# Rotary embedding on one core: ScalarE's copies and casts go to VectorE, GpSimd and the DMA queue

## The chip, the core and the metric

The kernel runs on one core of a Trainium2 chip. The metric is the device time of one execution in microseconds (us); the time of a kernel is the median of its runs. Three runs of the kernel before gave 316.24, 316.26 and 316.33 us.

## The reference

The input x has the shape 8 x 2048 x 16 x 64 (batch, position, head, element) in fp32. In each head the 64 elements are 32 pairs; pair i at position s is rotated by the table entries cos[s, i] and sin[s, i]:

```python
x1 = x_pairs[..., 0]
x2 = x_pairs[..., 1]
out1 = x1 * cos - x2 * sin
out2 = x1 * sin + x2 * cos
out = np.stack([out1, out2], axis=-1).reshape(batch, seq_len, num_heads, head_dim)
```

One of the 8 batches is 2048 x 1024 fp32 values, 8.39 MB. All of x is read once (67.1 MB) and an output of the same size is written once; the two tables are 0.26 MB each.

## The kernel before, in words

Position s = 16 p + k lies in partition p, row k of 16, so a batch is 128 partitions x 16 rows x 1024 elements, and each partition's 64 KB of a batch lie in one piece in DRAM. The data is held in SBUF as bf16. The tile `xt` has five homes of one batch each (32 KB a partition); batches 0 to 4 take homes 0 to 4, batches 5, 6 and 7 take homes 0, 1 and 2 again, once batches 0, 1 and 2 are stored.

All large transfers are issued by GpSimd (POOL in the profile) on one queue, and the DMA engines convert between fp32 in DRAM and bf16 in SBUF on the way: `load(b, n)` (line 63) brings in n batches, `store(b, n)` (line 67) takes n batches out. SyncE (SP) issues two transfers on its own queue, which does not convert: the head, the first 4 rows of batch 0 (line 92), and the tail, the last 4 rows of batch 7 (line 133). Both pass as fp32 through a staging tile `st`, and ScalarE (ACT) casts them (lines 101 and 132).

`rotate(b, k0, k1)` is three VectorE (DVE) instructions: qt = x times the sine table (line 82), x = x times the cosine table, in place (line 83), and x plus the pair-swapped qt, in place (line 88). Batch 0 is rotated in two parts (4 rows and 12 rows), every other batch in one. There is one work buffer, which `head`, `qt` and `tail` share in turn.

The order of the work is written out by hand; each engine follows the program's order, and a waiting instruction holds up everything behind it on its engine. What GpSimd does, in this order:

1. The loads of batch 0 (12 rows, line 93), cos and sin (lines 94, 95), batches 1 and 2 in one, batch 3 (both line 63), 14 rows of batch 4 (line 98) and its last 2 rows (line 99).
2. The store of batch 0 (line 67). Two ScalarE copies of one element hold it: line 111 reads an element of the 14 rows of batch 4, so it waits until these have landed, and line 112 rewrites the first element of batch 0 in place, so that the store has to wait for it.
3. `mark` (line 116), a GpSimd copy of the last element of batch 4, which waits for that load. It stands ahead of the store of batches 1 and 2.
4. The store of batches 1 and 2, the load of batch 5 (into home 0, so it waits until batch 0 is stored), the load of batches 6 and 7 (homes 1 and 2, so it waits for the store of batches 1 and 2).
5. The store of batches 3 and 4, the store of batches 5 and 6, and the first 12 rows of batch 7 (line 127).

At the end ScalarE's line 131 writes one element of batch 6's home, so that it waits until the store of batches 5 and 6 is done; then line 132 casts the tail, and SyncE stores it (line 133).

Of the kernel before, what the change touches and what calls it, by code (L numbers as in the profile page):

```python
# [2 lines left out]

# [4 lines left out]


@with_exitstack  # L10
def kernel(
    ctx: ExitStack,
    tc: tile.TileContext,
    x: bass.AP,
    cos: bass.AP,
    sin: bass.AP,
    out: bass.AP,
):
    nc = tc.nc
    fp32 = mybir.dt.float32  # L20
    bf16 = mybir.dt.bfloat16
    mult = mybir.AluOpType.mult
    add = mybir.AluOpType.add

    B, S, H, D = x.shape
    P = 128
    K = S // P
    KP = 16
    D2 = D // 2
    HD = H * D  # L30
    NX = 5
    HEAD = 4
    TAIL = 4
    LAST = 2


    HOME = [0, 1, 2, 3, 4, 0, 1, 2]

    x_t = x.rearrange("b (p k) h d -> b p k (h d)", p=P, k=K)
    out_t = out.rearrange("b (p k) h d -> b p k (h d)", p=P, k=K)  # L40
    x_r = x.rearrange("b (p k) h d -> p b (k h d)", p=P, k=K)
    out_r = out.rearrange("b (p k) h d -> p b (k h d)", p=P, k=K)
    cos_t = cos.rearrange("(p k) c -> p (k c)", p=P, k=K)
    sin_t = sin.rearrange("(p k) c -> p (k c)", p=P, k=K)

    consts = ctx.enter_context(tc.tile_pool(name="consts", bufs=1))
    stage = ctx.enter_context(tc.tile_pool(name="stage", bufs=1))

    xt = consts.tile([P, NX, K * HD], bf16)
    cos_sb = consts.tile([P, K * D2], fp32)  # L50
    sin_sb = consts.tile([P, K * D2], fp32)
    c_tab = consts.tile([P, K, D], bf16)
    s_tab = consts.tile([P, K, D], bf16)

    gate = consts.tile([1, 1], bf16)
    mark = consts.tile([1, 1], bf16)

    def home(b, k0=0, k1=K):
        return xt[:, HOME[b], k0 * HD : k1 * HD].rearrange("p (k c) -> p k c", c=HD)

    def load(b, n):
        h = HOME[b]
        nc.gpsimd.dma_start(out=xt[:, h : h + n], in_=x_r[:, b : b + n])  # L63

    def store(b, n):
        h = HOME[b]
        nc.gpsimd.dma_start(out=out_r[:, b : b + n], in_=xt[:, h : h + n])  # L67

    def rotate(b, k0=0, k1=K):
        nk = k1 - k0  # L70
        xp = home(b, k0, k1)
        qt = stage.tile([P, KP, HD], bf16, name="qt", tag="work")

        def rows(a):
            return a.rearrange("p k (h e) -> p k h e", h=H, e=D)

        def tab(a):
            return dataclasses.replace(
                a, offset=a.offset + k0 * D, ap=[a.ap[0], [D, nk], [0, H], [1, D]]
            )  # L80

        nc.vector.tensor_tensor(out=rows(qt[:, :nk]), in0=rows(xp), in1=tab(s_tab), op=mult)  # L82
        nc.vector.tensor_tensor(out=rows(xp), in0=rows(xp), in1=tab(c_tab), op=mult)  # L83
        q_swap = dataclasses.replace(
            qt, offset=qt.offset + 1, ap=[qt.ap[0], [2, nk * HD // 2], [-1, 2]]
        )
        x3 = xp.rearrange("p k (a j) -> p (k a) j", j=2)
        nc.vector.tensor_tensor(out=x3, in0=x3, in1=q_swap, op=add)  # L88

    with tc.manual_schedule():  # L90
        head = stage.tile([P, TAIL, HD], fp32, name="st", tag="work")
        nc.sync.dma_start(out=head[:, :HEAD], in_=x_t[0, :, :HEAD])
        nc.gpsimd.dma_start(out=home(0, HEAD), in_=x_t[0, :, HEAD:])  # L93
        nc.gpsimd.dma_start(out=cos_sb, in_=cos_t)  # L94
        nc.gpsimd.dma_start(out=sin_sb, in_=sin_t)  # L95
        load(1, 2)
        load(3, 1)
        nc.gpsimd.dma_start(out=home(4, 0, K - LAST), in_=x_t[4, :, : K - LAST])  # L98
        nc.gpsimd.dma_start(out=home(4, K - LAST), in_=x_t[4, :, K - LAST :])  # L99

        nc.scalar.copy(out=home(0, 0, HEAD), in_=head[:, :HEAD])  # L101
        s2 = s_tab.rearrange("p k (i j) -> p (k i) j", j=2)
        nc.vector.tensor_copy(out=s2[:, :, 0], in_=sin_sb)  # L103
        nc.vector.tensor_scalar_mul(s2[:, :, 1], sin_sb, -1.0)  # L104
        nc.vector.tensor_copy(  # L105
            out=c_tab.rearrange("p k (i j) -> p (k i) j", j=2),
            in_=cos_sb.to_broadcast([P, K * D2, 2]),
        )
        rotate(0, 0, HEAD)
        rotate(0, HEAD, K)  # L110
        nc.scalar.copy(out=gate, in_=home(4, K - LAST - 1, K - LAST)[:1, 0, :1])  # L111
        nc.scalar.copy(out=xt[:1, HOME[0], :1], in_=xt[:1, HOME[0], :1])  # L112
        store(0, 1)
        rotate(1)
        rotate(2)
        nc.gpsimd.tensor_copy(out=mark, in_=xt[:1, 4, K * HD - 1 :])  # L116
        store(1, 2)
        load(5, 1)
        load(6, 2)
        rotate(3)  # L120
        rotate(4)
        store(3, 2)
        for b in range(5, B):
            rotate(b)
            if b == 6:
                store(5, 2)
        nc.gpsimd.dma_start(out=out_t[B - 1, :, : K - TAIL], in_=home(B - 1, 0, K - TAIL))  # L127

        tail = stage.tile([P, TAIL, HD], fp32, name="st", tag="work")
        last = home(B - 1, K - TAIL, K)  # L130
        nc.scalar.copy(out=xt[:1, HOME[B - 2], :1], in_=xt[:1, HOME[B - 1], K * HD - 1 :])  # L131
        nc.scalar.copy(out=tail, in_=last)  # L132
        nc.sync.dma_start(out=out_t[B - 1, :, K - TAIL :], in_=tail)


# [1 line left out]
_INS = ['x', 'cos', 'sin']  # L137
_OUTS = [((8, 2048, 16, 64), 'float32')]


# [23 lines left out]
```

## Time and profile before

The profile is of one execution. Times in it are us from its first instruction.

| What | Value |
|---|---|
| median of the three runs | 316.26 us |
| span of the profiled execution, first to last instruction | 314.4 us |
| what lies around the span (median less span) | 1.8 us |
| DVE busy | 210.4 us, 30 instructions |
| ACT busy | 8.9 us, 6 instructions |
| POOL busy | 13.9 us, 19 instructions |
| DMA packets, bytes counted in the profile | 2816, 102.24 MB |
| share of the 16 DMA engines' span: GpSimd's queue, SyncE's queue | 96.8%, 3.3% |
| one rotation of a full batch (lines 82, 83, 88) | 3 x 8.69 us |
| ScalarE cast of the head, of the tail | 3.60 us each |
| GpSimd copy `mark` | 5.01 us |
| issue of one GpSimd transfer | 0.54 to 0.74 us |

How to read it: a DMA appears in three places. Its issue is a short instruction on the queue's engine (POOL, or SPq for SyncE); the page's last part gives the time from issue to landing; and the rows "GB/s" and "DMA" tell what the 16 DMA engines did meanwhile. Bytes are counted on the bf16 side for a converting load and on the fp32 side for a store, so that about 215 GB/s while loading and 430 GB/s while storing are the same pace in fp32 bytes. A window of the trace counts a DMA packet wholly where it starts.

### The profile page before, as it was taken

What the parts mean: (1) busy time and instruction counts of PE and PEld (TensorE: products, weight loads), DVE (VectorE), ACT (ScalarE), POOL (GpSimd) and SP (SyncE); (2) the same over time, 40 slices, a digit from 0 to 9 for tenths busy, and PEclk for the clock granted to TensorE, in tenths of its full rate; (3) what the DMA queues carried; (4) which work ended last, traced back from release to release, by engine and by line L of the source; (5) the groups of instructions that cost most, each with busy time, mean ns of one, the idle gap of its engine ahead of it and who ended that gap; (6) DMA issues with size and microseconds to landing.
All of it is one profiled execution on the core that took longest, in us unless ns stands there. A gap on an engine that the chain in (4) does not pass through costs nothing.

```text
span 314.4 us, 116 instructions
## 1 busy us (share of the span) xinstructions
DVE 210.4 (67%) x30; ACT 8.9 (3%) x6; POOL 13.9 (4%) x19
## 2 busy tenths in 40 slices
DVE  0009995099999999999992399903999999200000
ACT  1040000000000000000000000000000000000400
POOL 5000000000002400000000000000000000000000
DMA  7999999999999999999999999999999999999997
GB/s 254 263 283 200 200 200 267 200 200 213 229 233 258 425 509 400 400 459 475 400 200 246 221 200 200 254 213 333 400 525 409 400 400 525 409 400 400 434 434 333
DMA packets 2816, 102.24 MB, mean 325 GB/s; under 512 B 256, under 2 KB 256, under 8 KB 512
## 3 DMA queue, kind: packets, MB, share of 16 engines
q0 software_dynamic: 2528, 98.04, 96.8%
q1 hardware_dynamic: 288, 4.19, 3.3%
HBM read 67.63 MB, written 67.11 MB: 429 GB/s over the span
## 4 chain that ended last, share of the span: by engine, by line
another core or an unknown queue 87%; DMA 5%; ACT 1%; ACTq 1%; issue 0%
DMA st<-in_x_dram 5%; ACT xt L101 1%; ACTq L159 1%; ACT xt L131 0%; ACT xt L112 0%; ACTq L131 0%; ACT gate L111 0%
## 5 line engine op out<-in xcount | busy, mean ns | idle before, releaser
L82 DVE TENSOR_TENSOR qt<-xt,s_tab 128x16384 bf16<-128x16384 bf16 (+2 forms) x9 | 69.7, 7743 | 34.4 <-DMA xt<-in_x_dram 34.3
L83 DVE TENSOR_TENSOR xt<-xt,c_tab 128x16384 bf16<-128x16384 bf16 (+2 forms) x9 | 69.7, 7744 | 0.4
L88 DVE TENSOR_TENSOR xt<-xt,qt 128x16384 bf16<-128x16384 bf16 (+2 forms) x9 | 69.7, 7744 | 0.3
L103 DVE CAST s_tab<-sin_sb 128x512 bf16<-128x512 f32 x1 | 0.5, 458 | 23.8 <-DMA sin_sb<-in_sin_dram 23.8
L67 POOL DMA_DIRECT2D out_dram<-xt x4 | 2.7, 671 | 185.5 <-ACT xt L112 93.8
L131 ACT COPY xt<-xt 1x1 bf16<-1x1 bf16 x1 | 0.2, 193 | 195.4 <-DMA out_dram<-xt 195.4
L116 POOL COPY mark<-xt 1x1 bf16<-1x1 bf16 x1 | 5.0, 5014 | 1.4 <-DMA xt<-in_x_dram 1.4
L63 POOL DMA_DIRECT2D xt<-in_x_dram x4 | 2.6, 656 | 43.0 <-DMA out_dram<-xt 43.0
L101 ACT CAST xt<-st 128x4096 bf16<-128x4096 f32 x1 | 3.6, 3604 | 13.3 <-DMA st<-in_x_dram 13.3
L132 ACT CAST st<-xt 128x4096 f32<-128x4096 bf16 x1 | 3.6, 3598 | 0.0
L111 ACT COPY gate<-xt 1x1 bf16<-1x1 bf16 x1 | 0.2, 193 | 79.7 <-DMA xt<-in_x_dram 79.7
L127 POOL DMA_DIRECT2D out_dram<-xt x1 | 0.6, 572 | 25.5 <-DVE xt L88 25.5
L101 ACT ACT_TABLE_LOAD x1 | 1.3, 1283 | 0.7 <-PEq L148 0.7
L93 POOL DMA_DIRECT2D xt<-in_x_dram x1 | 0.7, 680 | 0.8 <-PEq L159 0.8
L105 DVE CAST c_tab<-cos_sb 128x1024 bf16<-128x1024 f32 x1 | 0.7, 684 | 0.0
L99 POOL DMA_DIRECT2D xt<-in_x_dram x1 | 0.6, 592 | 0.0
L98 POOL DMA_DIRECT2D xt<-in_x_dram x1 | 0.6, 586 | 0.0
L95 POOL DMA_DIRECT2D sin_sb<-in_sin_dram x1 | 0.6, 562 | 0.0
L94 POOL DMA_DIRECT2D cos_sb<-in_cos_dram x1 | 0.6, 554 | 0.0
L104 DVE TENSOR_SCALAR s_tab<-sin_sb 128x512 bf16<-128x512 f32 x1 | 0.4, 445 | 0.0
L112 ACT COPY xt<-xt 1x1 bf16<-1x1 bf16 x1 | 0.2, 189 | 0.0
L148 POOL MEMSET const-float32-0.0<- 128x1 f32 x1 | 0.1, 93 | 0.2 <-issue 0.2
(3 smaller groups left out, 0.3 us busy)
## 6 DMA issues: line engine op xcount, KB each, us to landing
xt<-in_x_dram POOLq DMA_DIRECT2D x2, 8192.0 KB, 58.5
xt<-in_x_dram POOLq DMA_DIRECT2D x2, 4096.0 KB, 67.6
out_dram<-xt POOLq DMA_DIRECT2D x1, 6144.0 KB, 40.9
xt<-in_x_dram POOLq DMA_DIRECT2D x1, 3584.0 KB, 94.3
xt<-in_x_dram POOLq DMA_DIRECT2D x1, 3072.0 KB, 21.2
st<-in_x_dram SPq DMA_DIRECT2D x1, 2048.0 KB, 14.5
out_dram<-st SPq DMA_DIRECT2D x1, 2048.0 KB, 15.5
xt<-in_x_dram POOLq DMA_DIRECT2D x1, 512.0 KB, 96.3
```

The source lines that it names most:

```text
L63: nc.gpsimd.dma_start(out=xt[:, h : h + n], in_=x_r[:, b : b + n])
L67: nc.gpsimd.dma_start(out=out_r[:, b : b + n], in_=xt[:, h : h + n])
L82: nc.vector.tensor_tensor(out=rows(qt[:, :nk]), in0=rows(xp), in1=tab(s_tab), op=mult)
L83: nc.vector.tensor_tensor(out=rows(xp), in0=rows(xp), in1=tab(c_tab), op=mult)
L88: nc.vector.tensor_tensor(out=x3, in0=x3, in1=q_swap, op=add)
L93: nc.gpsimd.dma_start(out=home(0, HEAD), in_=x_t[0, :, HEAD:])
L94: nc.gpsimd.dma_start(out=cos_sb, in_=cos_t)
L101: nc.scalar.copy(out=home(0, 0, HEAD), in_=head[:, :HEAD])
L105: nc.vector.tensor_copy(out=c_tab.rearrange("p k (i j) -> p (k i) j", j=2), in_=cos_sb.to_broadcast([P, K * D2, 2]),)
L116: nc.gpsimd.tensor_copy(out=mark, in_=xt[:1, 4, K * HD - 1 :])
L132: nc.scalar.copy(out=tail, in_=last)
L159: with _tile.TileContext(nc) as tc:
```

## The change

- The head's cast (line 101) is an instruction of VectorE, at the same place of the program.
- Batch 4 is loaded by one DMA on GpSimd's queue, not by two (14 rows and 2 rows).
- The two ScalarE copies that hold the first store are gone. In their place GpSimd copies the last element of batch 3 (home 3) ahead of the store, so the store waits, behind that copy on its own engine, until the load of batch 3 has landed.
- Batch 7 is stored by one DMA on GpSimd's queue. The tail's two ScalarE instructions, its staging tile and SyncE's transfer are gone; the 12-row store of line 127 becomes one of 16 rows at the same place.
- The loop over the last three batches is written out, in the same order. ScalarE has no instruction left.

```diff
-        head = stage.tile([P, TAIL, HD], fp32, name="st", tag="work")
+        head = stage.tile([P, HEAD, HD], fp32, name="st", tag="work")
...
-        nc.gpsimd.dma_start(out=home(4, 0, K - LAST), in_=x_t[4, :, : K - LAST])
-        nc.gpsimd.dma_start(out=home(4, K - LAST), in_=x_t[4, :, K - LAST :])
+        load(4, 1)
 
-        nc.scalar.copy(out=home(0, 0, HEAD), in_=head[:, :HEAD])
+        nc.vector.tensor_copy(out=home(0, 0, HEAD), in_=head[:, :HEAD])
...
         rotate(0, 0, HEAD)
         rotate(0, HEAD, K)
-        nc.scalar.copy(out=gate, in_=home(4, K - LAST - 1, K - LAST)[:1, 0, :1])
-        nc.scalar.copy(out=xt[:1, HOME[0], :1], in_=xt[:1, HOME[0], :1])
+        nc.gpsimd.tensor_copy(out=gate, in_=xt[:1, 3, K * HD - 1 :])
         store(0, 1)
...
-        for b in range(5, B):
-            rotate(b)
-            if b == 6:
-                store(5, 2)
-        nc.gpsimd.dma_start(out=out_t[B - 1, :, : K - TAIL], in_=home(B - 1, 0, K - TAIL))
-
-        tail = stage.tile([P, TAIL, HD], fp32, name="st", tag="work")
-        last = home(B - 1, K - TAIL, K)
-        nc.scalar.copy(out=xt[:1, HOME[B - 2], :1], in_=xt[:1, HOME[B - 1], K * HD - 1 :])
-        nc.scalar.copy(out=tail, in_=last)
-        nc.sync.dma_start(out=out_t[B - 1, :, K - TAIL :], in_=tail)
+        rotate(5)
+        rotate(6)
+        store(5, 2)
+        rotate(7)
+        store(7, 1)
```

More of the change, by code (lines that the diff above doesn't have):

```diff
@@ L32 @@
     HEAD = 4
-    TAIL = 4
-    LAST = 2
     HOME = [0, 1, 2, 3, 4, 0, 1, 2]
```

## The prediction

> **What bounds the kernel now.** I read the page's head and slices first, then the six DMA issues with their landings, then the busy time by stage, and last the timeline around the first store.
>
> ```profile
> span 314.4 us, 116 instructions
> DVE 210.4 (67%) x30; ACT 8.9 (3%) x6; POOL 13.9 (4%) x19
> ...
> DMA  7999999999999999999999999999999999999997
> ...
> HBM read 67.63 MB, written 67.11 MB: 429 GB/s over the span
> ```
>
> No engine is near its span, but the DMA row is 9 in all slices but the first and last. So the 16 DMA engines set the time: 134.7 MB in 314.4 us. The windows below are cut at landings: batch 3 loaded, batch 4 loaded (two DMAs), batches 1 and 2 stored, 3 and 4 stored, 5 and 6 stored, and batch 7 stored (two DMAs). The columns are window, length, busy time of DVE, ACT, POOL, clock, DMA share, GB/s.
>
> ```profile
> 62.40:81.70 19.30, 19.16 (x3) 0.00 (x0) 0.00 (x0) 1.00 0.99 214
> 81.70:101.10 19.40, 19.33 (x3) 0.29 (x2) 0.55 (x2) 1.00 1.03 247
> 121.00:159.40 38.40, 38.13 (x6) 0.00 (x0) 0.59 (x2) 1.00 1.02 423
> 217.00:255.60 38.60, 38.45 (x5) 0.00 (x0) 0.70 (x1) 1.00 1.02 435
> 255.60:294.20 38.60, 13.70 (x2) 0.00 (x0) 0.57 (x1) 1.00 1.00 428
> 294.20:313.60 19.40, 0.00 (x0) 3.69 (x2) 0.00 (x0) 1.00 0.92 392
> ```
>
> Every batch costs 19.2 to 19.4 us, loaded or stored, whole or in two pieces: 16 of these are 310 us, and the rest is the start and the end. VectorE waits for loads at 62.5, 178.4 and 217.0, and no transfer starts late. The last row's share of 0.92 isn't a hole: a window counts a packet where it starts, and 16 packets of 48 KB, 0.79 MB, had started just before 294.2 (19.4 us x 392 GB/s is 7.6 MB of the 8.39). In the trace's packet records 15 or 16 engines have a packet in flight from 2.3 us to 312.8 us. The queue serves its DMAs in the order of issue: the store of batches 3 and 4 is issued at 167.55, behind a load issued at 159.37, and lands 88.1 us later, at 255.6, 38.6 us after that load's 217.0. So a transfer issued early waits its turn, and all that counts is that each is issued before the queue runs dry. **An edit is worth only what it changes in DMA bytes, in cost per packet, or in a queue run dry.**
>
> **The change part by part.**
>
> *Head's cast on VectorE.* Removed: one ACT cast, 3.60 us (line 101), at 15.29. Added: a 128x4096 fp32 to bf16 cast on VectorE. No row shows that; the nearest are the DVE casts of 512 and 1024 elements, 0.458 and 0.684 us. Their difference gives 0.44 ns an element, so 2.0 us; 4 x 0.684 is 2.7 us; ACT's 3.60 is the upper end. I take 2.7: 15.3 to 18.0. VectorE's next instruction waits for sin until 23.84, and the rotation after it ends at 51.8, 10.7 us before batch 1 lands. Cost 0; even at 3.6 us it would end at 18.9.
>
> *Batch 4 in one DMA.* One issue less on POOL (0.59 us, at 4.78, nothing behind it): 0. In the queue, the packet records give per engine 8 packets every 2.112 us and 8 every 0.305 us, 19.33 us, where batch 3 has 8 every 2.412 us, 19.30 us. With one pair of end marks less this is **-0.05 us**; the rows' landings (19.4 against 19.3) say -0.1. Rotation 4 starts at 141.0, so the landing at about 101 isn't waited for by VectorE.
>
> *The gate.* The two ACT copies at 98.61 and 98.70 go; a GpSimd copy comes ahead of the first store.
>
> ```profile
> 79.93 8.69 DVE L88 TENSOR_TENSOR xt<-xt,qt 128x16384 bf16<-128x16384 bf16 x1
> 88.65 8.69 DVE L82 TENSOR_TENSOR qt<-xt,s_tab 128x16384 bf16<-128x16384 bf16 x1
> 97.38 8.69 DVE L83 TENSOR_TENSOR xt<-xt,c_tab 128x16384 bf16<-128x16384 bf16 x1
> ...
> 99.19 0.54 POOL L67 DMA_DIRECT2D out_dram<-xt  x1 [93.81 <-ACT xt L112]
> 101.10 5.01 POOL L116 COPY mark<-xt 1x1 bf16<-1x1 bf16 x1 [1.37 <-DMA xt<-in_x_dram]
> 106.11 8.69 DVE L88 TENSOR_TENSOR xt<-xt,qt 128x16384 bf16<-128x16384 bf16 x1
> ```
>
> The mark copies one element and takes 5.01 us: it begins within line 83 (97.38 to 106.07) and ends at 106.11, when that instruction has ended. So a GpSimd copy waits for the VectorE instruction in progress. The new gate waits for batch 3, issued at 3.7 and landing 78.0 us later, at 81.7, within line 88 of rotation 1. At best it takes some 0.2 us as on ACT (81.9); as the mark did, it ends at 88.65. I take 88.65, then 0.54 us of issue. Before, the store was issued at 99.19 and its first packets ran on from batch 4's last at 100.4 to 100.8, so the queue did not run dry; now it is queued 10 us earlier behind batch 4. Cost 0, cover 10 us. The Trainium skill (SBUF — State Buffer, Who interferes with whom) says that a VectorE instruction with two SBUF inputs and a GpSimd instruction that reads SBUF exclude each other, and whichever comes second is blocked until the first ends. By this rule the change swaps two ScalarE copies that wait for nobody for a blocked one; the sum stays, since 88.65 is in time.
>
> Behind the gate on POOL: the store's issue, the mark, and all later transfers. The mark still waits for batch 4 (101.0) and gets through at 106.1, the next store still waits for line 88 at 114.80, and its turn in the queue is 120. The load of batch 5 waits for the first store's landing, 121.0, with a turn at 158. All as before. If a copy makes VectorE wait instead, the row above prices it at 0.04 us (106.07 to 106.11), against 5 us of cover.
>
> *Batch 7 in one DMA.* The ACT copy, the 3.60 us cast, the SP issue and SyncE's 2 MB transfer go; the 12-row store, issued at 269.63, becomes 16 rows. Its turn comes at 293.5, so the earlier work is covered by 24 us. In the packet records the latest engine needs 19.39 us for batch 7 in two pieces (48 KB packets every 1.81 us, 16 KB ones every 0.61); eight whole 64 KB packets, one every 2.41 us and the last one's 2.45, make 19.31: **-0.07 us**. The end waits for a landing on GpSimd's queue, not SyncE's. From the last packet's end to the landing SyncE's took 0.3 us (313.23 to 313.55), GpSimd's 12-row store the same (310.19 to 310.53): 0, with bounds of -0.2 and +0.2 from the rounding of these.
>
> **Sum.** -0.05 - 0.07 = -0.12 us on a span of 314.4; the 1.8 us around it contain nothing that changes. On the median: **316.26 - 0.12 = 316.15 us**, no change within what this kernel's measurement can tell (0.2%, 0.63 us).
>
> **The rivals.**
>
> *The gate comes through late (slower).* If the copy doesn't get in between two VectorE instructions at 88.65, it is tried again at 97.35, which is just in time, and at 106.1, which isn't. From 99.5 on the queue runs dry at 100.7: copy to 106.1, issue from 106.4, first packet about 1.2 us after it (99.19 to 100.4, an upper bound), 107.6: +6.9 us, **323.1 us**. For it: VectorE runs without a gap from 62.5 to 167. Against it: the mark got in at the first border. 0.08.
>
> *The early store shares the DMA engines with batch 4 (slower).* If both were served in turn, batch 4 would land near 120 rather than 101, the mark behind it would end with the VectorE instruction in progress at 123.5, and the store of batches 1 and 2 would go out then, its packets from about 124.7 into a queue empty since 120.5: +4.2 us, **320.5 us**. Against it: the store issued at 167.55 took its turn. 0.05.
>
> *Fewer DMAs save more (faster).* If the 0.92 in the last window is waste, 8% of 19.4 us returns, 1.5 us: **314.7 us**. Against it: the packet records have no holes, and batch 4's last 512 KB landed 2.5 us after its first part (4.26 + 94.3, then 4.78 + 96.3), where one eighth of 19.3 us is 2.4. The Trainium skill (DMA: Bandwidth & Descriptors, Anatomy of one DMA — SWDGE) gives a DMA on this path a fixed cost of about 2.0 us besides its bytes; if that held in a full queue, two DMAs less would save 4 us, an estimate of 312.3. The 0.1 us beside it says that the fixed part is latency here, which the queue hides. 0.07.
>
> **How the numbers follow.** The forecast has 0.80, its own range 315.4 to 316.9: the sum's -0.12, the end's 0.2 either way, and some 0.4 for a small shift at one of the three changed places. This is also the range, as the rivals left out hold 0.20. Of the forecast's 0.80 I put 0.03 beyond 0.63 us on the fast side and 0.02 on the slow side: faster 0.10, same 0.75, slower 0.15.
>
> **What would show it.** Right: ACT's row gone; a DVE cast of about 2 to 3 us at 15.3; the gate's copy from 81.7 to 88.65 and the first store's issue by 89.5; the mark at 101 to 106.1 and the issue at 115.1 unchanged; load 5 issued at 121; DMA row all 9s, batch 7 landing 19.3 to 19.4 us after batch 6. Wrong: the gate at 97 or 106, a hole in the DMA row near 101 to 108, batch 4 landing much later than 101, or an end that comes more than 0.5 us after the last packet.

## The result, and the profile after

The changed kernel takes 317.64 us (median of 5 runs, 317.51 to 317.85) against 316.26 us: 1.0042 times the kernel before, 95% interval 1.0031 to 1.0053. It is **1.4 us slower**, where no measurable change was forecast, and outside the range given. The profiled execution has a span of 315.9 us where before had 314.4.

Line numbers of the changed kernel are 2 lower than before's in `rotate`, `load` and `store` (lines 80, 81, 86, 61, 65); the gate is line 108, the mark line 112. The page's head and DMA row look as before:

```profile
span 315.9 us, 106 instructions
...
DVE 212.6 (67%) x31; POOL 19.1 (6%) x19
...
DMA  8999999999999999999999999999999999999996
```

ScalarE is gone, and the DMA row still has 9 everywhere but at the ends. The packet records (the trace's start and length of every DMA packet) show no hole: from 5.5 to 312 us an engine is without a packet for 0.03 us on average, as in the kernel before. The windows cut at landings, as in the prediction (batch 4 loaded, batch 0 stored, batches 1 and 2 stored, 3 and 4 stored, 5 and 6 stored, 7 stored; with no ACT column now):

```profile
81.70:102.10 20.40, 20.33 (x3) 7.41 (x2) 1.00 1.00 231
102.10:121.50 19.40, 19.33 (x3) 4.67 (x2) 1.00 1.01 432
121.50:160.20 38.70, 38.39 (x6) 0.56 (x1) 1.00 1.01 420
218.00:256.70 38.70, 38.51 (x5) 0.71 (x1) 1.00 1.01 434
256.70:295.30 38.60, 13.65 (x2) 0.57 (x1) 1.00 1.02 435
295.30:314.60 19.30, 0.00 (x0) 0.00 (x0) 1.00 0.89 380
```

One stage has grown: batch 4's load takes 20.4 us where it took 19.4. All later stages are what they were, to 0.1 us. To the hundredth, batch 4 lands at 102.09 (before 101.04: +1.05) and the stores of batches 5 and 6 at 295.28 (294.23: +1.05). The last packet ends at 314.21 (313.23: +0.98, so batch 7 in one DMA is 0.07 us cheaper). From the last landing to the end of the span there are 1.30 us (314.57 to 315.88), where there were 0.86 (313.57 to 314.43: +0.44). 0.98 and 0.44 are the whole difference of 1.4 us. There are **two losses**, at different places.

The timeline around the gate is what the prediction expected:

```profile
81.72 6.92 POOL L108 COPY gate<-xt 1x1 bf16<-1x1 bf16 x1 [76.87 <-DMA xt<-in_x_dram]
88.59 0.54 POOL L65 DMA_DIRECT2D out_dram<-xt  x1
...
102.14 3.95 POOL L112 COPY mark<-xt 1x1 bf16<-1x1 bf16 x1 [13.01 <-DMA xt<-in_x_dram]
```

The gate's copy waits for VectorE and ends in the gap at 88.6, and the store is issued 12 us before its turn. What follows isn't. Narrower windows of the changed kernel (the last column, GB/s, and the share before it count packets where they start) show the last packets of batch 4's load:

```profile
95.40:97.80 2.40, 2.37 (x2) 0.00 (x0) 1.00 1.01 218
97.80:98.30 0.50, 0.50 (x1) 0.00 (x0) 1.00 6.84 1049
98.30:101.10 2.80, 2.80 (x1) 0.00 (x0) 1.00 0.00 0
101.10:101.90 0.80, 0.80 (x1) 0.00 (x0) 1.00 3.07 1311
```

All 16 engines start their last packet of the load between 97.8 and 98.3, and the next one, the first of the store, only after 101.1, not 2.4 us later. By the packet records these last packets take 3.09 to 3.61 us where the seven before them take 2.43; the mean excess is 1.0 us. (Excess or stretch, from here on: by how much these last packets are longer than packets of their size elsewhere, on average over the 16 engines.) There is no hole: the engines are "busy" all along, only slower. The next place where a store lies queued behind a load is at 217 us:

```profile
214.60:215.10 0.50, 0.00 (x0) 0.00 (x0) 1.00 3.95 852
215.10:217.00 1.90, 0.00 (x0) 0.00 (x0) 1.00 0.24 52
217.00:217.60 0.60, 0.00 (x0) 0.00 (x0) 1.00 3.83 1638
```

Here the next packets start at 217.0 to 217.6, 2.4 us after the last ones: no stretch, though that store had been queued for 49 us. In the kernel before, neither place has a stretched packet. Its lines there (with the ACT column):

```profile
99.00:100.00 1.00, 1.00 (x1) 0.00 (x0) 0.54 (x1) 1.00 0.99 201
100.00:101.00 1.00, 1.00 (x1) 0.00 (x0) 0.00 (x0) 1.00 2.84 1126
101.00:102.00 1.00, 1.00 (x1) 0.00 (x0) 0.90 (x1) 1.00 0.00 0
216.00:217.00 1.00, 0.00 (x0) 0.00 (x0) 0.00 (x0) 1.00 2.45 1049
```

Batch 4's last 4 KB packets all take 0.32 us, and the first store's 16 first packets start at 100.4 to 100.8, right behind them.

### The profile page after: what moved, and what is told of

Its sections match the earlier page's. It is cut to its first block, busy times and chain, and to the rows that moved or that the text cites. A ratio compares the mean times of both kernels' runs of the same rounds, so it can differ in the third digit from the quotient of the medians.

```text
span 315.9 us, 106 instructions
## 1 busy us (share of the span) xinstructions
DVE 212.6 (67%) x31; POOL 19.1 (6%) x19
## 2 busy tenths in 40 slices
DMA packets 2528, 102.24 MB, mean 324 GB/s; under 512 B 224, under 2 KB 224, under 8 KB 352
## 4 chain that ended last, share of the span: by engine, by line
DVE 58%; another core or an unknown queue 11%; issue 9%; DMA 7%; POOL 1%; POOLq 0%; DVEq 0%; PEldq 0%
DVE xt L81 19%; DVE xt L86 19%; DVE qt L80 19%; DMA sin_sb<-in_sin_dram 7%; POOL out_dram L65 0%; POOL xt L91 0%; POOLq L149 0%; DVE c_tab L102 0%; POOL cos_sb L92 0%; DVE s_tab L100 0%; DVE s_tab L101 0%; DVEq L80 0%; DVEq L81 0%; PEldq L149 0%
## 5 line engine op out<-in xcount | busy, mean ns | idle before, releaser
L98 DVE CAST xt<-st 128x4096 bf16<-128x4096 f32 x1 | 2.3, 2294 | 15.3 <-DMA st<-in_x_dram 15.3
L108 POOL COPY gate<-xt 1x1 bf16<-1x1 bf16 x1 | 6.9, 6922 | 76.9 <-DMA xt<-in_x_dram 76.9
L61 POOL DMA_DIRECT2D xt<-in_x_dram x5 | 3.1, 641 | 44.4 <-DMA out_dram<-xt 44.4
L112 POOL COPY mark<-xt 1x1 bf16<-1x1 bf16 x1 | 4.0, 3952 | 13.0 <-DMA xt<-in_x_dram 13.0
L91 POOL DMA_DIRECT2D xt<-in_x_dram x1 | 0.7, 682 | 0.8 <-PEq L149 0.8
```

Of the source, the lines that this page charges most:

```text
L98: nc.vector.tensor_copy(out=home(0, 0, HEAD), in_=head[:, :HEAD])
L108: nc.gpsimd.tensor_copy(out=gate, in_=xt[:1, 3, K * HD - 1 :])
```

## The experiments

"After" is the changed kernel, "before" the kernel before; before's median in the shared runs was 316.22 to 316.40 us. The ratio of each run is to before, with its 95% interval. Each run has one profile; seven of them (3, 4, 7, 12, 13, 14 and 16) also show passing stretches of 0.2 to 0.8 us in all, somewhere between 47 and 96 us, ahead of the places that the argument is about. What causes these is not known.

**Which part costs it.** First run: before, with the new gate alone.

```diff
-        nc.scalar.copy(out=gate, in_=home(4, K - LAST - 1, K - LAST)[:1, 0, :1])
-        nc.scalar.copy(out=xt[:1, HOME[0], :1], in_=xt[:1, HOME[0], :1])
+        nc.gpsimd.tensor_copy(out=gate, in_=xt[:1, 3, K * HD - 1 :])
```

> The kernel before, with only the gate changed: GpSimd's copy on batch 3 in place of ScalarE's two copies; batch 4 stays in two DMAs, the tail stays. After's trace shows the last packet of batch 4 stretched from 2.43 to 3.1-3.6 us on all 16 engines (about +1.02 us), and 0.44 us more between the last landing and the end. Theory EARLY (a store queued behind a load stretches that load's last packets, whatever their size): 316.26 + 1.0 = 317.3 us, the stretch now in the last 4 KB packets. Rival WHOLE (the stretch comes with the large last packet; small ones don't suffer): 316.3 us, no stretch.

Measured: 317.23 us, 1.0022 (1.0012 to 1.0033). WHOLE falls. The DMA issues of this run's page:

```profile
xt<-in_x_dram POOLq DMA_DIRECT2D x1, 3584.0 KB, 94.3
...
xt<-in_x_dram POOLq DMA_DIRECT2D x1, 512.0 KB, 97.4
```

The 14 rows land as before (94.3 us after their issue), the last 2 rows 97.4 us after theirs where it was 96.3: 102.18 us. The 4 KB packets of the last rows now take up to 0.89 us instead of 0.32. So the loss comes with the gate alone, and it sits in the last 2.4 us of the load, whatever its packets.

Second: after, with batch 4's load in two DMAs again.

```diff
+    LAST = 2
...
-        load(4, 1)
+        nc.gpsimd.dma_start(out=home(4, 0, K - LAST), in_=x_t[4, :, : K - LAST])
+        nc.gpsimd.dma_start(out=home(4, K - LAST), in_=x_t[4, :, K - LAST :])
```

> The changed kernel, with batch 4 loaded by two DMAs (14 and 2 rows) as before; gate on batch 3 and the one store of batch 7 stay. EARLY: 317.6 us, as the changed kernel. WHOLE: about 316.6 us, the 1.0 us gone and the 0.44 us at the end left.

Measured: 317.72 us, 1.0042 (1.0030 to 1.0055), batch 4 at 102.21. As EARLY expects; the split isn't what protected before.

Third: after, with the tail as before (ScalarE's cast and SyncE's store).

```diff
+    TAIL = 4
...
-        store(7, 1)
+        nc.gpsimd.dma_start(out=out_t[B - 1, :, : K - TAIL], in_=home(B - 1, 0, K - TAIL))
...
+        nc.scalar.copy(out=tail, in_=last)
+        nc.sync.dma_start(out=out_t[B - 1, :, K - TAIL :], in_=tail)
```

> The changed kernel, with the store of batch 7 in two pieces as before (12 rows on GpSimd's queue, 4 rows cast by ScalarE and stored by SyncE). Theory END (SyncE's list of final waits ends with SyncE's own transfer; with the last landing at the head of the list, five more wait instructions run after it): 317.64 - 0.4 = 317.2 us, 0.86 us from last landing to the end of the span. Rival: the two-piece store costs 0.07 us more and saves nothing: 317.7 us. EARLY and WHOLE expect the stretch of 1.0 us at 98 to 101.7 us to stay.

Measured: 317.34 us, 1.0027 (1.0017 to 1.0038), 0.30 less than after; 0.86 us from the last landing (314.56) to the end of the span (315.42). The size is near what END expected; that its reason is not what sets the time is shown below, with the list of waits. The stretch stayed (batch 4 at 102.04).

Fourth: after, with no gate: the line with the gate's copy is deleted.

> The changed kernel without any gate: the first store is issued when batch 0 is rotated, at about 52 us, with three batches of loads ahead of it in the queue. EARLY and WHOLE: 317.6 us, the last packet of batch 4 stretched as with the gate. Theory COPY (the stretch comes from the blocked GpSimd copy and the issue just after it at 88.6 us): no stretch, about 316.6 us. Theory NEAR (it comes from an issue that arrives while few packets are left in the queue): no stretch either, about 316.6 us.

Measured: 317.68 us, 1.0040 (1.0027 to 1.0054). The store is issued at 52.08, batch 4 lands at 102.11, and 0.99 us of excess lies in the same last packets. COPY and NEAR fall: the stretch needs neither the blocked copy nor an issue with few packets left. A load is slowed by the store that lies behind it, and only at its end.

**Why there and not at 217 us.** VectorE was idle at 217 us. Fifth run: after, with VectorE kept busy there.

```diff
+        qd = stage.tile([P, KP, HD], bf16, name="qd", tag="work")
+        for _ in range(2):
+            nc.vector.tensor_tensor(out=qd, in0=home(5), in1=home(5), op=mult)
         rotate(6)
```

> The changed kernel, with two more VectorE multiplications of a full batch (batch 5 squared into the work buffer, unused) ahead of the rotation of batch 6, so that VectorE is busy at the second place where a load is followed by a queued store (215 to 218 us), as it is at the first (98 to 102 us); there it was idle and no packet was stretched. Theory VECTOR (the stretch needs a busy VectorE): a second stretch of about 1.0 us at 214 to 218 us, 318.6 us. Theory FIRST (it belongs to the first store of the program): no second stretch, 317.6 us; the later rotation is covered.

Measured: 317.60 us, 1.0043 (1.0028 to 1.0058); no stretched packet near 215 us, 0.91 us at 98. VECTOR falls.

Sixth: after, with a small store ahead of all others.

```diff
+        early = consts.tile([P, 256], bf16)
+        nc.vector.memset(early, 0.0)
+        nc.gpsimd.dma_start(out=out_t[0, :, 0, :256], in_=early)
         load(1, 2)
```

> The changed kernel, with a small store (128 x 1 KB of zeros, overwritten later by the store of batch 0) on GpSimd's queue between the load of sin and the load of batches 1 and 2. FIRST: the stretch moves to this store at about 22 to 24 us and is gone at 98 to 102 us. If it is paid there in full: 317.9 us (0.3 us for the bytes); if it is hidden beside SyncE's queue or smaller packets: down to 316.9 us. VECTOR, or a theory by place in the queue: the stretch stays at 98 to 102 us, 317.9 us.

Measured: 317.64 us, 1.0047 (1.0030 to 1.0063). The small store costs 0.37 us (batches 1 and 2 land at 62.73, in after at 62.36), and the stretch at 98 us is halved: 0.49 us. In the seven profiles with 32 KB packets at the end of that load and no earlier store (after, runs 3, 4, 5, 7, 9 and 10) it is 0.77 to 1.16 us. Neither the form of FIRST that was expected (gone) nor the rival (unchanged) is met; the runs below on the place in the queue and on the size settle which it leans to.

Seventh: after, with one more place where a store follows a load.

```diff
-        store(1, 2)
-        load(5, 1)
-        load(6, 2)
+        store(1, 1)
+        load(5, 1)
+        store(2, 1)
+        load(6, 1)
+        load(7, 1)
```

> The changed kernel, with the store of batches 1 and 2 and the load of batches 6 and 7 cut in single batches and ordered store 1, load 5, store 2, load 6, load 7: one more place where a queued store follows a load, at about 160 us, with VectorE busy and a single-batch store. FIRST: no stretch there, about 317.6 us. VECTOR: a second stretch of 1.0 us at 158 to 161 us, 318.6 us. Theory SINGLE (it belongs to a store of a single batch behind a load): a stretch there too, 318.6 us.

Measured: 317.75 us, 1.0047 (1.0032 to 1.0062). Batch 5 lands at 159.99 and no packet is stretched there; at 98 us it is 0.77. SINGLE falls, and VECTOR again.

**The place in the queue, or the first store?** The small store also moved all later entries of the queue by 9 (2672 packets on the page where after has 2528, 16 engines). So the ninth run moves them without a store:

```diff
-        nc.gpsimd.dma_start(out=sin_sb, in_=sin_t)
+        for i in range(2):
+            c = slice(i * 256, (i + 1) * 256)
+            nc.gpsimd.dma_start(out=sin_sb[:, c], in_=sin_t[:, c])
```

> The changed kernel, with the load of sin cut into two DMAs, so that every later DMA stands 9 entries further in the queue of each DMA engine, as it did behind the small early store, which halved the stretch (1.0 to 0.5 us). Theory FIRST (the stretch belongs to the first store): batch 4 lands at 102.1 us or a little later, 1.0 us stretched, 317.7 us. Theory PLACE (it depends on how many entries went through the queue before): the stretch is 0.5 us as with the early store.

Measured: 317.70 us, 1.0039 (1.0019 to 1.0059), batch 4 at 102.38, 1.16 us of excess. The tenth cuts both tables in four in the same way:

> The changed kernel, with the loads of cos and sin cut into four DMAs each: 54 entries further. FIRST: 1.0 us stretched at the end of batch 4's load, some 0.3 us later for the small packets. PLACE: the stretch is gone or at another packet.

Measured: 320.63 us, 1.0139 (1.0109 to 1.0168). The stretch is where it was, at the end of batch 4's load (1.14 us). The run is slower because batches 1 and 2 land at 64.94 where after has 62.36, and its page shows why:

```profile
L95 POOL DMA_DIRECT2D sin_sb<-in_sin_dram x4 | 2.2, 559 | 17.2 <-DMA xt<-in_x_dram 17.2
```

The last of the small pieces, issued at 22.88, is the ninth DMA that GpSimd issues, and it waited 17.2 us, until the first (batch 0) had landed. The loads behind it were issued only from 23.41 on, where after has 3.01. So the queue ran dry around 24 us (1.5 us without a packet, on average over the engines), and the first packets of batches 1 and 2 took 2.89 to 3.38 us, 0.74 us too long, with no store in the queue. A stretch of this kind is therefore not a store's alone.

PLACE falls, though more weakly than planned: the pages count only 16 and 96 packets more than after in these two runs (2544 and 2624), where the small store added 144, and that the queue counts 9 and 54 entries is not shown. The next run has the same 2672 packets as the sixth.

Eleventh: the early store four times as large (`[P, 1024]`, and 1024 elements of each row).

> The changed kernel, with the early store of zeros four times as large (128 x 4 KB, 0.5 MB, 1.2 us of the queue). FIRST in the form 'a first touch that is paid by bytes or addresses': the stretch at 98 us falls below 0.5 us. PLACE: 0.5 us, as with 128 x 1 KB, which has the same number of entries.

Measured: 318.26 us, 1.0062 (1.0039 to 1.0085). The stretch at the end of batch 4's load is gone, which with the same count of packets PLACE can't explain. This run's windows there (everything is 1.67 us later, by what the early store costs):

```profile
96.60:98.60 2.00, 2.00 (x1) 0.00 (x0) 1.00 1.22 262
98.60:99.10 0.50, 0.47 (x2) 0.00 (x0) 1.00 0.00 0
99.10:101.00 1.90, 1.90 (x1) 0.00 (x0) 1.00 1.28 276
101.00:101.70 0.70, 0.70 (x1) 0.00 (x0) 1.00 0.00 0
101.70:103.50 1.80, 1.80 (x1) 0.77 (x1) 1.00 1.36 583
```

Packets start in bursts, 97.2 to 97.5, 99.6 to 100.0 and, the store's first, 102.0 to 102.4: 2.4 us apart, as if nothing were there. But the stretch has moved, not vanished: 15 of the 16 last packets of batch 0's load take 1.94 to 2.41 us in place of 1.83, on average 0.37 us more. They start 3.6 us ahead of the early store's first packets (19.9 against 23.5), with the two short table loads in between. In after and in the small-store run none of them is stretched. So in these runs a load in flight shortly ahead of the first sizeable store pays, and pays less if that store is smaller.

Twelfth: the small store on SyncE's queue instead (fp32 zeros, `nc.sync.dma_start`).

> The changed kernel, with the early store (128 x 1 KB of fp32 zeros) on SyncE's queue, not on GpSimd's, just behind the head's load. FIRST, if what is first is the output's memory: the stretch at 98 us is 0.5 us or less. FIRST, if it is the first store of GpSimd's queue: the full 1.0 us. PLACE: the full 1.0 us.

Measured: 317.93 us, 1.0051 (1.0031 to 1.0071), batch 4 at 102.36, 0.64 us of excess at 98. Below the full 1.0, but not the 0.5 of GpSimd's small store, and this profile has other slightly stretched packets from 47 to 80 us. Inconclusive on which queue matters.

Fifteenth: the 4 KB store into batch 3's part of the output.

```diff
-        nc.gpsimd.dma_start(out=out_t[0, :, 0, :1024], in_=early)
+        nc.gpsimd.dma_start(out=out_t[3, :, 0, :1024], in_=early)
```

> The changed kernel, with the early store of 128 x 4 KB of zeros into batch 3's part of the output, not batch 0's. Into batch 0's part it took the stretch at 98 us away (1.0 to 0.0). Theory ADDRESS (what is touched first is that part of the output's memory): the full 1.0 us is back at 98 us, 319.2 us. Theory ONCE (what counts is that a store of some size has run before, wherever): no stretch at 98 us, 318.2 us.

Measured: 318.32 us, 1.0063 (1.0048 to 1.0079), no stretch at 98 us, 0.39 us on batch 0's last packets. ADDRESS falls, ONCE holds: it isn't the part of the output's memory, but that a store has run before.

**From which lead on.** In before, ScalarE's gate sets the first store's issue by the size of batch 4's second DMA; only `LAST` was changed, to 4, 3 and 1 rows (eighth, thirteenth, fourteenth run).

> The kernel before, with batch 4 cut at 12 and 4 rows, not 14 and 2: ScalarE's gate lets the first store go at about 96.3 us, 2.4 us earlier, with some 4.8 us of loads ahead of it. Theory EARLY in its plain form (any store queued before the last packets of the load start): the full 1.0 us, 317.3 us. Theory NEAR (the issue must come some 7 us or more ahead, as at 88.6): 316.3 us.

> The kernel before, with batch 4 cut at 13 and 3 rows: the first store's issue moves from 99.2 to about 98.0 us, 2.7 us before the load's end (before: 1.5 us, no stretch; cut at 12 rows: 3.9 us, batch 4 landed at 102.01, the full 1.0 us). If the loss begins when the store is there while the engines still read the load from DRAM, part of it: 316.4 to 317.1 us. If it is a step by some fixed time: either 316.3 or 317.2 us.

> The kernel before, with batch 4 cut at 15 and 1 rows: the first store's issue at about 100.4 us, 0.3 us before the load's end. The queue runs dry for about 0.5 us (issue to first packet took at most 1.2 us): 316.8 us. If the gate at 14 rows still loses something that no packet record shows, this one is no slower than before: 316.2 us.

| rows in the second DMA | first store issued | batch 4 lands | batch 0 is stored | median | ratio to before |
|---|---|---|---|---|---|
| 4 | 96.74 us | 102.01 us | 121.42 us | 317.17 us | 1.0031 (1.0018 to 1.0044) |
| 3 | 98.28 us | 101.38 us | 120.79 us | 316.64 us | 1.0011 (1.0002 to 1.0020) |
| 2 (before) | 99.19 us | 101.04 us | 120.44 us | 316.26 us | 1 |
| 1 | 100.65 us | 101.28 us | 121.62 us | 317.36 us | 1.0034 (1.0022 to 1.0047) |

An issue 4.3 us before the load's undisturbed landing (101.04) costs the full 1.0 us at the landing; at 1.8 us it costs nothing. NEAR falls again. The run with 3 rows (2.8 us) looks like a third of the loss, but its packets say otherwise: batch 4's last ones, of 6 KB, take 0.47 us each, 0.01 us of excess in all. The 0.34 us were lost earlier, by one of the passing stretches: packets of its 13 rows that start between 83 and 88 us take up to 2.20 us in place of 1.98, 0.28 us in all, and the store is issued only at 98.28 (98.0 was expected). In this profile the first store costs nothing at 2.8 us. The 11 times of this run go from 316.25 to 317.20 us, so its other executions may differ. Whether the loss is a step between 2.8 and 4.3 us isn't shown.

With 1 row the queue runs dry: the store's first packets start 1.1 us after its issue (at 101.8), when the load's packets are through at about 100.9. That is a hole of 0.9 us where 0.5 was expected; 0.24 us of a passing stretch stand ahead of it. The loss is 1.1 us. So before's cut is the fastest of these four: later the queue runs dry, and much earlier the load is slowed.

**The end.** Sixteenth run: before, with only batch 7's store made one DMA on GpSimd's queue.

> The kernel before, with only the store of batch 7 made one DMA on GpSimd's queue. Theory DRAIN (GpSimd's final drain ends 0.57 to 0.83 us after its queue's last landing in every run; before, SyncE's tail lands 3 us later and hides that): 1.25 us from the last landing to the end in place of 0.81, 316.26 + 0.44 - 0.07 = 316.6 us. Rival LIST (only the place in SyncE's list of final waits counts): the same time if the last landing is near the head of the list, 0.06 us less for each place further.

Measured: 316.63 us, 1.0012 (1.0003 to 1.0021): DRAIN's number. Its profiled execution was the longest of its 11 (packets were stretched between 49 and 91 us), so only its end is read. There each engine runs instructions named DRAIN and then a barrier. The trace's view of the last line, of before, after and this run: count and min/median/max in ns of GpSimd's drains, starts of the first and the last.

```profile
L159 POOLq DRAIN  x3: 45/87/41561, 269.6 to 314.2; - x3
```

```profile
L149 POOLq DRAIN  x3: 45/96/44498, 270.7 to 315.6; - x3
```

```profile
L153 POOLq DRAIN  x3: 45/82/44530, 270.4 to 315.3; - x3
```

GpSimd's first drain of the end begins when its last store is issued and lasts until 311.17 in before, 315.15 in after, 314.91 here: 0.62, 0.58 and 0.62 us after the last landing of its own queue (310.55, 314.57, 314.29). In the experiments this is 0.58 to 0.66 us, and 0.82 in the tenth. The final barrier, where the engines wait for each other, needs it. In before, SyncE's tail lands at 313.57, 2.4 us after GpSimd's drain has ended, and the barrier goes on 0.17 us later; in after it waits for the drain: SyncE is through its own waits at 314.98, GpSimd's drain ends at 315.15, and the barrier goes on at 315.20, 0.63 us after the landing. LIST falls: in the seventh run SyncE's remaining waits after the last landing took 0.27 us where after's took 0.41, and its end came 1.37 us after the landing all the same. But SyncE's list is only just hidden: if GpSimd's drain took no time, after's list would still end some 0.25 us later behind its landing than before's (0.41 less 0.15 us, an estimate).

## Why the prediction was wrong

**The gate.** Its failed sentence is "Cost 0, cover 10 us." The gate itself did what the prediction said, to 0.1 us: copy ended at 88.6, issue at 88.59, nothing late behind it on POOL or VectorE. What failed is the step under it: "a transfer issued early waits its turn, and all that counts is that each is issued before the queue runs dry". The row it was read from, the store of batches 3 and 4, is the third store of the queue. Runs 1, 4 and 8 show that the first store, once queued 4 us or more ahead, costs the load in front of it 1.0 us; runs 5, 7, 11 and 15 that later ones don't. So this term was +1.0 us, not 0. The rival "the early store shares the DMA engines with batch 4" had the right sign and place with a far too large price (batch 4 at 120 us rather than 102.09): it supposed packets served in turn, and the packets kept their order.

What happens inside the DMA engines isn't shown. The Trainium skill (DMA: Bandwidth & Descriptors, Two DMAs through the same engine are not ordered) says that descriptors of one engine's queue start in order but are pipelined, and that its read and write sides are separate queues. That the loss came at a lead of 4.3 us and not at 1.8, and is smaller where the store is, would agree with a read side that goes on to the store while the load's last data is still being written; no run tests this. It doesn't explain why only the first store costs, nor the stretched loads of run 10. The cause inside the engines stays open.

**The end.** Its failed term is "0, with bounds of -0.2 and +0.2". The landings agree with it (0.34 us from last packet to landing in before, 0.36 in after). The term stopped at the landing: what comes between it and the end of the span, GpSimd's drain of 0.6 us, was hidden behind SyncE's tail and became the last thing: +0.44 us where 0 was put. The trace of before already had 0.86 us behind its last landing, which the prediction didn't look into. "The 1.8 us around it contain nothing that changes" holds (317.64 less 315.88 is 1.76); the loss is within the span.

**The small terms.** Batch 7 in one DMA: -0.07 forecast, 1.05 - 0.98 = 0.07 measured. The head's cast: 2.7 us taken, 2.29 measured, ended at 17.6, hidden as said. Batch 4 in one DMA: -0.05 (the two figures that it rests on, 19.33 and 19.30, give -0.03 and an estimate for the end marks) is near the limit of what the runs resolve: with two DMAs it lands at 102.18 and 102.21 (runs 1 and 2), with one at 102.09 and 102.04 (after and run 3). The rival "the gate comes through late" did not happen. "Fewer DMAs save more" fell: batch 7 saved 0.07 us, and batch 4 some 0.1 us at most. The Trainium skill (DMA: Bandwidth & Descriptors, Anatomy of one DMA — SWDGE) gives a fixed cost of about 2.0 us for a DMA on GpSimd's path, which for two DMAs would be 4 us, an estimate. These runs show none of that saved where other work stands in the queue. (One of the two DMAs that went was SyncE's, not GpSimd's.) The sum itself is off by a rounding: 316.26 - 0.12 is 316.14.

**The sum, corrected:** gate with the merged load +1.05, batch 7 in one DMA -0.07, drain +0.44: +1.4 us on 316.26, 317.7 us. None of the experiments points to a kernel faster than before.

## What to carry to other kernels

Where the DMA queue is the bound, "issued early" isn't free by itself: look at the packets of the transfer in front when a store joins the queue for the first time. Here that issue was best at about 1.8 us before the load's landing, of the four leads tried: late enough to leave the load alone, early enough that the queue did not run dry. Before counting a term at nothing because a like one costs nothing later in the trace, ask what was the first of its kind. And follow the end past the last landing to the last instruction: here, what the barrier waited for changed with the queue that landed last. When a run disagrees by a few tenths, look in its packets for the place where the time went before putting it down to the edit: the run with 3 rows would have been misread.

## What the runs showed that was not expected

- A first store queued 4 us or more ahead of its turn behind loads slows these loads' last packets by 1.0 us in all (2.43 to 3.1-3.6 us each), without a hole in the DMA row. An early store of 128 x 1 KB halves it, one of 128 x 4 KB moves it forward to that store and cuts it to 0.4 us.
- GpSimd's drain at the end lasts until 0.58 to 0.82 us after its queue's last landing, in every run.
- When the queue runs dry, a GpSimd store's first packet starts 1.1 us after its issue (100.65 to 101.8).
- Cutting the two 256 KB table loads in eight 64 KB ones cost 2.6 us: GpSimd's ninth DMA waited 17.2 us for its first to land, and the queue ran dry.
